# A transformer layer on one core: the first token block alone, from forgetting attention to its expert rows, under the other three; two dense expert blocks for three

## The chip, the cores and the metric

The kernel runs on one core of one Trainium2 chip. The metric is the device time in microseconds (us) of one execution. Before the change the median of three runs is 5321.05 us (5316.64 to 5322.71). The engines of a core are called as in its profile: PE (TensorE, matmuls; PEld is its weight load), DVE (VectorE), ACT (ScalarE), POOL (GpSimd) and SP (SyncE, which here only issues transfers).

## The reference

One layer over 512 tokens of 2048 features, in fp32, with a memory of 256 rows. Cut to what matters here:

```python
h = hybrid_mixer(x, w_in, ...)            # x @ w_in -> mLSTM (4 heads) and forgetting attention (16 heads of 128)
                                          # merged = sigmoid(g_ml) * (h @ w_br_ml) + sigmoid(g_fx) * (y @ w_br_fox)
                                          # return merged @ w_out
x = layer_norm(DN_ALPHA * x + h, ...)
h = memory_cross_attention(x, mem, w_q, w_kv, w_o)
x = layer_norm(DN_ALPHA * x + h, ...)
h = peer_ffn(x, w_pq, sub_keys, expert_u, expert_v)
x = layer_norm(DN_ALPHA * x + h, ...)

def peer_ffn(...):
    q = (x @ w_pq).reshape(B, S, PEER_HEADS, 2, PEER_DK // 2)       # 8 heads, two half keys
    sc = jnp.einsum('bshpd,hpnd->bshpn', q, sub_keys)               # 128 sub-keys each
    top_s, top_i = lax.top_k(sc, PEER_TOPK)                         # 16 + 16, then 16 of the 256 pairs
    ...
    def block(args):                                                # per block of 128 tokens
        a = jnp.einsum('tkd,td->tk', expert_u[it], xt)              # 8 * 16 = 128 experts a token
        hact = gelu(a) * gt
        return jnp.einsum('tk,tkd->td', hact, expert_v[it])
```

There are 128 x 128 = 16384 experts, each with one row of 2048 in `peer_u` and one in `peer_v` (128 MB a table). A token uses 128 of them. So a block of 128 tokens can be done in two ways: by gathering each token's own rows, or densely, with all 16384 experts and gates that are zero for those not chosen.

The forgetting attention is causal: the first 128 tokens need only the keys and values of the first 128. The mLSTM carries its state from the first token to the last.

## The kernel before

Tokens stand in four blocks of 128 (TB = 4). Weights come from memory in pieces of [128 x 1024] fp32, 512 KB, one `dma_start` on SP's queue each (`load_raw`, L116 to L119, tile `raw`, three buffers). Matmuls run in a rounded fp32 format; to keep precision, each weight piece is split in two (`split`, L110 to L114): ACT casts the high part (L111: `whi`, `vh`, `hph`), DVE subtracts it from the piece for the low part (L114: `wlo`, `vl`, `hpl`), or POOL does (L113), when the caller says so. `load_w` (L121) does load and split with two buffers each for `whi` and `wlo`. `mm3` (L128 to L131) multiplies with three matmuls: high by high (L129), and the two mixed products (L130, L131). Two functions use them for a group of 512 output features (eight pieces of weight): `group_ws` (L133) gives the features on the partitions and all tokens in the columns, 24 matmuls a piece; `group_as` (L147) gives a token block on the partitions and 512 features in the columns, 6 matmuls a piece and block.

The stages, in order: x and the gates; mLSTM (20 groups and its recurrence); forgetting attention (L354 on: 12 groups for queries, keys and values, `fox_head` at L358, four groups of gates, four of `w_br_fx`); `w_out` with norm 1 (L449 on), beside which the memory's keys and values are made (`w_xkv`, eight groups with 256 columns); the query groups and cross-attention; `w_xo` and norm 2; `peer_wq` with the selection (`top16` L619, `select` L628, `soften` L664).

Then the experts. Three token blocks (NDENSE = 384) are dense, the fourth is gathered.

- `stage_a(c)` (L785): gelu of `peer_u` by the dense tokens for first key c, 128 experts: two pieces `uT` of 512 KB and 48 matmuls of 384 columns. The first 52 run ahead (LOOK); most of the results wait in DRAM (`gad`).
- Beside these the gates are made as a dense array [second key, first key, token] (L705 to L745): in steps of four tokens, DVE compares the selected keys with a row of numbers (L724, L726, tiles of 128x512), POOL multiplies with the gate in two halves (L729), PE multiplies (L734), ACT and DVE copy and add the halves (L740, L741), and the result goes to DRAM (`gd`).
- `stage_h(c)` (L802): activation times gate (L813, tile `gb`), and its split (`hph`, `hpl`).
- `stage_o(c0, dh, fill)` (L842): J = 4 first keys at a time and one half of the 2048 output columns: four pieces of `peer_v` (tile `vh`, `vl`), 18 matmuls of 512 columns each into six PSUM banks, which DVE adds to the accumulators `acc` in SBUF (L879). Between these, `fill` starts the remaining `stage_a` and the gathers.
- The gathered block: each of 128 `gather_u` fetches with one indirect DMA on POOL's queue (L820) one row of `peer_u` for each of the block's 128 tokens, 1 MB, into `rows` (two buffers), and DVE multiplies and sums it with the token's features (L830); each `gather_v` does so with `peer_v` and adds the row times its factor to the accumulator (L839). u rows of one batch of eight and v rows of the batch before alternate. They are spread over the loop and tied to its pace by `pace` (L765).

The order of the instructions on each engine is chosen by the framework's scheduler, which simulates the program from the order in which it is written and the dependencies; there is no order written out by hand beside that and the `pace` ties. What a queue holds runs in its order: SP's queue carries the weight pieces, the gates and the output, POOL's carries its arithmetic and the gathers.

Of the kernel before, what the change touches and what calls it, by code (L numbers as in the profile page):

```python
# [21 lines left out]
P = 128  # L22
# [9 lines left out]
NDENSE = 384  # L32
# [4 lines left out]
# column groups of w_in, 512 columns each  # L37
# [6 lines left out]
def build(tc, I, out, dbg=None):  # L44
    nc = tc.nc
    dbg = dbg or {}
    with ExitStack() as ctx:
# [4 lines left out]
        apool = ctx.enter_context(tc.tile_pool(name="acts_a", bufs=1))  # L52
        phase_a = ctx.enter_context(ExitStack())
        bpool = phase_a.enter_context(tc.tile_pool(name="acts_b", bufs=1))
# [29 lines left out]
        # causal, transposed: [s, t] is one where t >= s  # L84
# [4 lines left out]
        # [q, k]: NEG where k > q  # L89
# [17 lines left out]
        lnbT = const_in("ln_bT", [P, 3, 16])  # L107

# [24 lines left out]
        def group_ws(src, X, n, evac, pool=False):  # L133
            """out^T of 512 features: evac(sub-block, bank [128 features, n tokens])."""
# [12 lines left out]
        def group_as(src, X, nt, evac):  # L147
            """512 features, tokens on partitions: evac(token block, bank [128 tokens, 512])."""
# [13 lines left out]
        def rstd(o, var, t):  # L162
            """o = (var + eps) ** -0.5, with one Newton step; t: two like columns of scratch."""
# [9 lines left out]
        # ================= x, gates =================  # L173
# [4 lines left out]
        with tc.tile_pool(name="gates", bufs=1, reuse_waits="tile") as gp:  # L178
# [21 lines left out]
            # log_sigmoid(z) = min(z, 0) - log1p(exp(-|z|))  # L200
# [4 lines left out]
            # log1p(e) = log(u) + (e - (u - 1)) / u  # L205
# [7 lines left out]
            # mLSTM: g = i - F, M = max(0, running max of g), m = F + M  # L213
# [15 lines left out]
        if "F" in dbg:  # L229
            nc.sync.dma_start(dbg["F"], sc_fx)  # L230
            nc.sync.dma_start(dbg["M"], sc_ml)

        wi = I["w_in"]

        # ================= mLSTM =================
        hT = []
        mg = dp.tile([16, P, S], F32, tag="mg", name="mg")
        with tc.tile_pool(name="ml", bufs=1, reuse_waits="tile") as mp:
            def mt(tag, bufs, shape=(P, 512)):
                return mp.tile(list(shape), F32, tag=tag, bufs=bufs, name=nm(tag))  # L240

            for h in range(ML_H):
# [59 lines left out]
                for tb in range(TB):  # L302
# [5 lines left out]
                    # r = 1 / max(|den|, exp(-m)); the head norm of num * r  # L308
# [23 lines left out]
            # sigmoid(g_ml) * (h @ w_branch_ml), transposed, to scratch  # L332
# [13 lines left out]
        if "mg" in dbg:  # L346
            nc.sync.dma_start(dbg["mg"], mg)
        if dbg.get("stop") == 1:
            return

        # ================= forgetting attention =================
        yT = []
        sgf = []
        with tc.tile_pool(name="fx", bufs=1, reuse_waits="tile") as fp:  # L354
            def ft(tag, bufs, shape=(P, 512)):
                return fp.tile(list(shape), F32, tag=tag, bufs=bufs, name=nm(tag))

            def fox_head(h, qT, kT, vts, off):  # L358
                nF = ft("nF", 2)
                nc.gpsimd.dma_start(nF, sc_fx[h].partition_broadcast(P))  # L360
                pr = []
                for qb in range(TB):
                    n = (qb + 1) * P
                    bank = sm_bank()
                    nc.tensor.matmul(bank[:, :n], qT[:, qb * P:n], kT[:, :n], start=True, stop=False)
                    nc.tensor.matmul(bank[:, qb * P:n], identb, maskb, start=False, stop=True)
                    p = fp.tile([P, n], F32, tag=f"p{qb}", bufs=1, name=nm("p"))
                    st = fp.tile([P, 4], F32, tag="st", bufs=8, name=nm("fst"))
                    nc.vector.tensor_tensor_reduce(out=p, in0=bank[:, :n], in1=nF[:, :n], scale=1.0, scalar=-3.0e38,
                                                   op0=ALU.add, op1=ALU.max, accum_out=st[:, 0:1])  # L370
                    nc.vector.tensor_scalar(st[:, 1:2], st[:, 0:1], -1.0, None, op0=ALU.mult)
                    nc.scalar.activation(p, p, AF.Exp, bias=st[:, 1:2], accum_out=st[:, 2:3])
                    nc.vector.reciprocal(st[:, 3:4], st[:, 2:3])
                    nc.vector.tensor_scalar(p, p, st[:, 3:4], None, op0=ALU.mult)
                    pr.append(p)
                pts = []
                for kb in range(TB):
                    bank = sm_bank()
                    for qb in range(kb, TB):
                        nc.tensor.transpose(bank[:, (qb - kb) * P:(qb - kb + 1) * P], pr[qb][:, kb * P:(kb + 1) * P],  # L380
                                            ident)
# [16 lines left out]
            for qd in range(4):  # L398
# [6 lines left out]
                def ev_k(s, b, ks=ks):  # L405
                    ks[s] = ft("c", 17)
                    nc.vector.tensor_copy(ks[s], b)
# [601 lines left out]
```

## Time and profile before

| | |
|---|---|
| median of three runs | 5321.05 us |
| the profiled execution's own span | 5323.6 us |
| PE busy | 5128.4 us, 24353 matmuls |
| DVE busy | 3192.8 us |
| ACT busy | 1594.5 us |
| POOL busy | 858.1 us |
| moved by DMA | 963.45 MB, 181 GB/s in the mean |

One execution on the chip was recorded. The page gives the busy time of each engine, slices of the span with the busy share in tenths, the DMA queues, the chain of work that ended last, and groups of instructions: line, engine, operation, tiles (written from read), shapes, their number, then busy time and the mean of one in ns, then the idle time of the engine just before them with what ended it. In a table of windows each row is a stretch of the span (from:to in us, length, then busy time and number of instructions for PE, PEld, DVE, ACT and POOL, the granted TensorE clock, the DMA share and GB/s). Ends of matmuls are modelled, and a matmul's mean includes what it overlaps with its neighbours, so its price is better read from a stretch in which PE never stops.

### The profile page before, as it was taken

The numbers are of one execution on the slowest core, as the hardware profiler recorded it, in microseconds if no ns is written. First come the engines' busy times: TensorE is split into PE (matmuls) and PEld (weight loads), VectorE is DVE, ScalarE is ACT, GpSimd is POOL, SyncE is SP. The second block draws the span as 40 slices with busy tenths as digits, with TensorE's granted clock in tenths as the row PEclk, the third lists the DMA queues.
The fourth block names the chain that finished last, engine by engine and source line by source line (L and its number), as shares of the span: only waits on it lengthen the run. The fifth ranks groups of instructions, "written<-read, shape, count | busy, mean of one in ns | idle before, by whom it ended". The sixth has DMA issues, their size and how long they took to land. (4 is left out here: it accounts for less than half of the span.)

```text
span 5323.6 us, 62349 instructions
## 1 busy us (share of the span) xinstructions
PE 5128.4 (96%) x24353; PEld 4366.2 (82%) x24353; DVE 3192.8 (60%) x4755; ACT 1594.5 (30%) x2260; POOL 858.1 (16%) x636
## 2 busy tenths in 40 slices
PE   9999999999999999999989978799999999999997
PEld 7777788877778888887878877788888888888886
DVE  4444322233332344632359999956888888888887
ACT  3322222222223222432232344333223332323232
POOL 0000000000000000500034544411122222222221
PEclk9999999999999999999999999999999999999998
DMA  3222233322222343632342344466888999999995
GB/s 132 86 89 84 87 111 107 108 87 91 90 89 89 113 135 127 207 126 75 100 141 84 118 138 143 157 226 233 323 326 330 341 325 337 331 333 334 336 342 207
DMA packets 295751, 963.45 MB, mean 181 GB/s; under 512 B 28604, under 2 KB 110076, under 8 KB 262304
## 3 DMA queue, kind: packets, MB, share of 16 engines
q1 hardware_dynamic: 178272, 597.37, 32.5%
q0 software_dynamic: 49552, 311.59, 15.9%
q10 hardware_dynamic: 67632, 50.50, 2.9%
q8 instruction: 191, 3.13, 0.2%
q14 instruction: 104, 0.85, 0.0%
HBM read 892.60 MB, written 66.76 MB: 180 GB/s over the span
## 5 line engine op out<-in xcount | busy, mean ns | idle before, releaser
L114 DVE TENSOR_TENSOR wlo<-raw,whi 128x1024 fp32r<-128x1024 f32 x748 | 978.4, 1308 | 1426.7 <-ACT whi L111 1399.7
L111 ACT CAST whi<-raw 128x1024 fp32r<-128x1024 f32 x768 | 809.9, 1055 | 2058.0 <-PE mm L130 868.4
L131 PE MATMUL pa<-Ah,wlo 128*128 128x384 f32 x2048 | 703.2, 343 | 80.0 <-DVE wlo L114 76.6
L129 PE MATMUL pa<-Ah,whi 128*128 128x384 f32 x2048 | 697.0, 340 | 19.4 <-ACT whi L111 16.9
L130 PE MATMUL mm<-Al,whi 128*128 128x512 f32 x1792 | 708.4, 395 | 3.6 <-DVE Al L114 3.6
L129 PE MATMUL mm<-Ah,whi 128*128 128x512 f32 x1792 | 707.7, 396 | 0.8 <-ACT whi L111 0.8
L130 PE MATMUL pa<-Al,whi 128*128 128x384 f32 x2048 | 695.5, 340 | 0.0
L131 PE MATMUL mm<-Ah,wlo 128*128 128x512 f32 x1792 | 677.6, 394 | 2.1 <-POOL wlo L113 1.6
L130 PE MATMUL po<-vl,hph 128*128 128x512 f32 x1536 | 602.2, 392 | 0.8 <-DVE vl L114 0.8
L131 PE MATMUL po<-vh,hpl 128*128 128x512 f32 x1536 | 600.7, 392 | 0.0
L129 PE MATMUL po<-vh,hph 128*128 128x512 f32 x1536 | 594.9, 391 | 4.3 <-ACT hph L111 2.7
L131 PEld LDWEIGHTS pa<-Ah,wlo 128*128 128x128 f32 x2048 | 391.5, 191 | 103.7 <-DVE wlo L114 97.1
L111 ACT CAST vh<-raw 128x1024 fp32r<-128x1024 f32 x256 | 269.4, 1053 | 631.4 <-DMA raw<-in_peer_v 444.3
L130 PE MATMUL mm<-wlo,Ah 128*128 128x512 f32 x1088 | 433.9, 399 | 0.3 <-DVE wlo L114 0.3
L131 PE MATMUL mm<-whi,Al 128*128 128x512 f32 x1088 | 424.0, 390 | 0.0
L129 PEld LDWEIGHTS pa<-Ah,whi 128*128 128x128 f32 x2048 | 391.8, 191 | 28.3 <-ACT whi L111 20.7
L130 PEld LDWEIGHTS mm<-Al,whi 128*128 128x128 f32 x1792 | 337.6, 188 | 81.1 <-issue 9.6
L131 PEld LDWEIGHTS mm<-Ah,wlo 128*128 128x128 f32 x1792 | 337.3, 188 | 75.1 <-POOL wlo L113 2.5
L129 PEld LDWEIGHTS mm<-Ah,whi 128*128 128x128 f32 x1792 | 337.9, 189 | 72.5 <-issue 1.7
L130 PEld LDWEIGHTS pa<-Al,whi 128*128 128x128 f32 x2048 | 391.3, 191 | 4.2
L129 PE MATMUL mm<-whi,Ah 128*128 128x512 f32 x1088 | 373.3, 391 | 0.7 <-ACT whi L111 0.7
L830 DVE SCALAR_TENSOR_TENSOR rows<-rows,x2l 128x2048 f32<-128x2048 f32 x128 | 292.9, 2289 | 130.9 <-DMA rows<-in_peer_u,ei 130.7
(297 smaller groups left out, 7477.9 us busy)
## 6 DMA issues: line engine op xcount, KB each, us to landing
raw<-in_w_in SPq DMA_DIRECT2D x256, 512.0 KB, 3.3
raw<-in_uT SPq DMA_DIRECT2D x256, 512.0 KB, 4.6
raw<-in_peer_v SPq DMA_DIRECT2D x256, 512.0 KB, 6.8
raw<-in_w_xkv SPq DMA_DIRECT2D x64, 512.0 KB, 3.3
gd<-stage ACTq DMA_DIRECT2D x12, 2048.0 KB, 13.4
G<-gd SPq DMA_DIRECT2D x64, 384.0 KB, 6.9
gad<-ga ACTq DMA_DIRECT2D x126, 192.0 KB, 4.8
gb<-gad SPq DMA_DIRECT2D x126, 192.0 KB, 6.2
```

What stands on the lines that cost most here:

```text
L111: nc.scalar.copy(hi, src)
L114: return nc.vector.tensor_sub(lo, src, hi.bitcast(F32))
L129: nc.tensor.matmul(o, wh, xh, start=first, stop=False)
L130: nc.tensor.matmul(o, wh, xl, start=False, stop=False)
L131: nc.tensor.matmul(o, wl, xh, start=False, stop=last)
L830: nc.vector.scalar_tensor_tensor(rows, rows, 1.0, x2l, op0=ALU.mult, op1=ALU.mult, accum_out=d[:, k % GB:k % GB + 1])
```

## The change

- The dense expert blocks are blocks 1 and 2 (`DENSE = (1, 2)`, NDENSE = 256). Blocks 0 and 3 are gathered.
- The memory's keys and values are made before the mLSTM and wait in DRAM.
- After the mLSTM, block 0 alone goes through forgetting attention, `w_br_fx`, `w_out`, norm 1, cross-attention, `w_xo`, norm 2, `peer_wq` and the selection. It loads the 36 groups of these stages (288 pieces) with `group_as` for one block, 6 matmuls of 512 columns a piece. Its keys and values of each head group wait in DRAM for the other blocks.
- Then the other three blocks go through the same 36 groups (384 columns in `group_ws`, three blocks in `group_as`), the pieces loaded a second time. With each of these pieces `load_w` issues 258/272 of a job of block 0's gathered expert part: one gather and its DVE product (all 128 of `peer_u`, then all 128 of `peer_v`, then the final norm). Each gather is tied to the split of the last piece. Every third split goes to POOL (`share=3`).
- The gates of the two dense blocks are built token by token: two DVE instructions on a [128 x 128] tile and one fp32 matmul a token, ACT copies the result; POOL has no part.
- `stage_a` runs with 256 columns; its first 20 first keys send their splits to POOL (before, the first four). In `stage_o` the two dense blocks take four banks, and the split of every third of four pieces goes to POOL. Block 3 is gathered in the loop with `rows` in three buffers, all u rows before the v rows, and starts after four first keys instead of eight.

The core of the diff (new or changed lines):

```diff
-NDENSE = 384
+DENSE = (1, 2)
+NDENSE = 128 * len(DENSE)
...
+        work = {"jobs": None, "rate": 0.0, "due": 0.0, "n": 0, "share": 0, "last": None}
...
-            split(hi, lo, raw, pool)
+            work["n"] += 1
+            if work["share"] and work["n"] % work["share"] == 0:
+                pool = True
+            work["last"] = split(hi, lo, raw, pool)
+            if work["jobs"] is not None:
+                work["due"] += work["rate"]
+                while work["due"] >= 1 and work["jobs"] is not None:
+                    work["due"] -= 1
+                    if next(work["jobs"], None) is None:
+                        work["jobs"] = None
             return hi, lo
...
+        def gather_rows(table, ei, k, last):
+            rows = gat.tile([P, D], F32, tag="rows", bufs=3, name=nm("rows"))
+            i = nc.gpsimd.indirect_dma_start(out=rows, out_offset=None, in_=I[table],
+                                             in_offset=bass.IndirectOffsetOnAxis(ap=ei[:, k:k + 1], axis=0))
+            after(i, last())
+            return rows
+
+        def gathered(t, xacc, ei, gg, last):
...
+            for k in range(P):
+                rows = gather_rows("peer_u", ei, k, last)
+                nc.vector.scalar_tensor_tensor(rows, rows, 1.0, xacc, op0=ALU.mult, op1=ALU.mult,
+                                               accum_out=dots[:, k:k + 1])
+                yield True
+            nc.scalar.mul(xacc, xacc, ALPHA)
+            nc.scalar.activation(dots, dots, AF.Gelu)
+            nc.vector.tensor_mul(dots, dots, gg)
+            for k in range(P):
+                rows = gather_rows("peer_v", ei, k, last)
+                nc.vector.scalar_tensor_tensor(xacc, rows, dots[:, k:k + 1], xacc, op0=ALU.mult, op1=ALU.add)
+                yield True
...
+            def proj(w, X, out, func=None, scale=1.0):
...
+                group_as(w, X, 1, ev)
+                return out
...
+            for qd in range(4):
+                tq = proj(wi[16 + 3 * qd], XA, big("tq"), scale=FX_D ** -0.5)
+                tk = proj(wi[17 + 3 * qd], XA, big("tk"))
+                vt = proj(wi[18 + 3 * qd], XA, big("vt"))
+                nc.gpsimd.dma_start(kvd[qd, 1], vt)
...
+        work.update(jobs=gathered(0, xacc0, ei0, gg0, lambda: work["last"]), rate=258 / 272, share=3)
...
+                group_ws(wi[16 + 3 * qd], XB, TR, ev_q)
+                group_ws(wi[17 + 3 * qd], XB, TR, ev_k)
+                group_as(wi[18 + 3 * qd], XB, 3, ev_v)
...
-                    nc.vector.tensor_tensor(o1, *i1, op=ALU.is_equal)
...
-                    nc.vector.tensor_tensor(e0, *i0, op=ALU.is_equal)
...
-                    nc.gpsimd.tensor_mul(o0, e0.unsqueeze(2).to_broadcast(f4),
-                                         gT[:, ta:ta + 4].bitcast(F32).unsqueeze(3).to_broadcast(f4))
...
+                    for u in range(4):
+                        c = slice(ta + u, ta + u + 1)
+                        o1 = gp.tile([P, P], F32, tag="o1", bufs=4, name=nm("o1"))
+                        nc.vector.tensor_scalar(o1, iota, selT["i1"][:, c], None, op0=ALU.is_equal)
+                        o0 = gp.tile([P, P], F32, tag="o0", bufs=4, name=nm("o0"))
+                        nc.vector.tensor_scalar(o0, iota, selT["i0"][:, c], selT["g"][:, c],
+                                                op0=ALU.is_equal, op1=ALU.mult)
+                        nc.tensor.matmul(bank[:, u * P:(u + 1) * P], o1, o0, start=True, stop=True)
...
-                uh, ul = load_w(I["uT"][c, kt], pool=c < 4)
+                uh, ul = load_w(I["uT"][c, kt], pool=c < 20)
...
-        LATE = 8          # first keys before the gathered block starts
+        LATE = 4
...
-                split(vh, vl, raw)
+                split(vh, vl, raw, pool=j == 2)
```

More of the change, by code (lines that the diff above doesn't have):

```diff
@@ new lines, in build, with fin_load, fin_stats @@
+        fst = {}
+        def fin_load(pool):
+            lw = []
+            for n in ("ln_w", "ln_b"):
+                t = pool.tile([P, D], F32, tag="rows", bufs=3, name=nm("lw"))
+                nc.gpsimd.dma_start(t, I[n][2].partition_broadcast(P))
+                lw.append(t)
+            return lw
+        def fin_stats(pool, t, acc, gs):
+            if t not in fst:
+                fst[t] = gat.tile([P, 32], F32, tag="fst", bufs=4, name=nm("fst"))
+            for g in gs:
+                nc.vector.bn_stats(fst[t][:, 6 * g:6 * g + 6], acc[:, g * 512:(g + 1) * 512])
@@ L694, in a_bank @@
+        work["share"] = 0
+        while work["jobs"] is not None:
+            if next(work["jobs"], None) is None:
+                work["jobs"] = None
         def a_bank():
@@ L727, in build @@
[L727 to L741 removed]
+                    bank = o_bank()
@@ L900, in fin @@
[L900 to L915 removed]
+                        fin(DENSE[t], acc[t], lwd)
```

841 lines of the change are left out of this document (457 added, 384 removed).

## The prediction

> **What bounds the kernel now.** I read the page first: its busy times and its slices.
>
> ```profile
> span 5323.6 us, 62349 instructions
> PE 5128.4 (96%) x24353; PEld 4366.2 (82%) x24353; DVE 3192.8 (60%) x4755; ACT 1594.5 (30%) x2260; POOL 858.1 (16%) x636
> DVE  4444322233332344632359999956888888888887
> GB/s 132 86 89 84 87 111 107 108 87 91 90 89 89 113 135 127 207 126 75 100 141 84 118 138 143 157 226 233 323 326 330 341 325 337 331 333 334 336 342 207
> ```
>
> PE is at 96%, but the slices show two halves: up to slice 20 DVE and the memory are mostly idle, in the last third both are near full. So I cut the span at the stage borders (the first weight cast of each stage) and asked for the windows: length, PE, PEld, DVE, ACT, POOL, granted clock, DMA share, GB/s.
>
> ```profile
> 0.00:945.00 945.00, 935.60 (x4097) 752.82 (x4098) 356.33 (x588) 259.04 (x306) 14.68 (x34) 1.00 0.29 99
> 945.00:1928.00 983.00, 983.00 (x4388) 792.37 (x4387) 346.05 (x609) 263.05 (x392) 18.30 (x34) 1.00 0.29 97
> 1928.00:2089.00 161.00, 160.05 (x706) 131.91 (x705) 60.80 (x69) 35.06 (x36) 8.60 (x16) 1.00 0.40 133
> 2089.00:2301.00 212.00, 201.16 (x1264) 181.57 (x1263) 128.52 (x132) 91.36 (x104) 74.66 (x60) 0.99 0.57 193
> 2301.00:2508.00 207.00, 207.00 (x886) 164.23 (x885) 61.31 (x86) 56.08 (x83) 0.00 (x0) 1.00 0.24 83
> 2508.00:2698.00 190.00, 190.00 (x830) 154.90 (x830) 62.52 (x76) 40.41 (x48) 6.46 (x12) 1.00 0.32 106
> 2698.00:2918.00 220.00, 202.22 (x935) 166.98 (x934) 180.89 (x607) 68.27 (x90) 105.11 (x80) 0.95 0.33 113
> 2918.00:3552.00 634.00, 534.76 (x2931) 500.46 (x2930) 563.32 (x1096) 249.25 (x561) 272.88 (x139) 0.97 0.46 151
> 3552.00:5293.00 1741.00, 1713.88 (x8328) 1520.63 (x8328) 1410.64 (x1458) 527.68 (x634) 347.17 (x259) 0.99 0.87 317
> 5293.00:5323.60 30.60, 0.76 (x4) 0.30 (x2) 22.46 (x43) 4.33 (x6) 10.24 (x3) 0.55 0.25 103
> ```
>
> They are mLSTM, forgetting attention, w_out, memory keys and values, query, w_xo, selection, look-ahead with gates, the expert loop, the tail. Up to 2918 PE bounds and DVE works a third of the time; the loop has PE, DVE and DMA at 98, 81 and 87%. Sums below stand against this span, 2.6 us (0.05%) above the median 5321.05.
>
> What a matmul costs is read where PE never stops, and with them the highest DMA rate and a stretch in which POOL works beside DVE:
>
> ```profile
> 1760.00:1920.00 160.00, 160.00 (x708) 132.53 (x707) 59.53 (x67) 37.94 (x44) 6.46 (x12) 1.00 0.37 116
> 2200.00:2222.00 22.00, 22.00 (x185) 22.00 (x185) 10.09 (x11) 8.38 (x8) 0.95 (x2) 1.00 0.73 255
> 3520.00:3555.00 35.00, 35.00 (x204) 35.00 (x203) 15.04 (x19) 11.44 (x16) 5.33 (x10) 1.00 1.01 369
> 2125.00:2215.00 90.00, 79.63 (x640) 77.64 (x639) 68.29 (x59) 40.08 (x50) 72.51 (x56) 0.98 0.64 216
> ```
>
> 512 columns: 160/708 = 0.226 us; 256: 22/185 = 0.119; 384: 35/204 = 0.172, while the memory gave 369 GB/s. Other prices are from the groups of instructions (mean ns of one behind the busy time), the DMA issues (us to landing last), and the loop's waits (us, times, longest):
>
> ```profile
> L111 ACT CAST whi<-raw 128x1024 fp32r<-128x1024 f32 x768 | 809.9, 1055 | 2058.0 <-PE mm L130 868.4 <-PE mm L131 627.1 <-DMA raw<-in_uT 244.0
> L114 DVE TENSOR_TENSOR vl<-raw,vh 128x1024 fp32r<-128x1024 f32 x256 | 311.2, 1219 | 39.3 <-ACT vh L111 33.1 <-PE pa L131 6.1
> L839 DVE SCALAR_TENSOR_TENSOR acc<-rows,dots,acc 128x2048 f32<-128x2048 f32 x128 | 300.6, 2348 | 89.4 <-DMA rows<-in_peer_v,ei 89.3
> L830 DVE SCALAR_TENSOR_TENSOR rows<-rows,x2l 128x2048 f32<-128x2048 f32 x128 | 292.9, 2289 | 130.9 <-DMA rows<-in_peer_u,ei 130.7
> L879 DVE TENSOR_TENSOR acc<-acc,po 128x512 f32<-128x512 f32 x372 | 238.6, 680 | 12.0 <-PE po L131 12.0
> L813 DVE TENSOR_TENSOR gb<-gb,G 128x384 f32<-128x384 f32 x126 | 69.0, 552 | 22.8 <-DMA gb<-gad 19.7 <-issue 2.4 <-DVE wlo L114 0.7
> L113 POOL TENSOR_TENSOR wlo<-raw,whi 128x1024 fp32r<-128x1024 f32 x20 | 47.9, 2393 | 29.4 <-ACT whi L111 29.3
> L374 DVE TENSOR_SCALAR p<-p,fst 128x128 f32<-128x128 f32 x16 | 4.6, 287 | 0.6
> ```
> ```profile
> raw<-in_w_in SPq DMA_DIRECT2D x256, 512.0 KB, 3.3
> raw<-in_peer_v SPq DMA_DIRECT2D x256, 512.0 KB, 6.8
> rows<-in_peer_u,ei POOLq DMA_INDIRECT x128, 8.8
> ```
> ```profile
> POOL rows L820 <- DVE rows L830: 618.5, 115, 9.6
> ACT vh L111 <- DMA raw<-in_peer_v: 444.3, 141, 8.2
> ```
>
> **The change, part by part.**
>
> *Memory keys and values first.* The 64 loads leave the norm beside which they ran: 384 matmuls with 512 columns and 768 with 256 are 384×0.226 + 768×0.119 = 178 us; with 12 us for the spill and the border (my choice; 0 to 30), behind 945: **1135**.
>
> *Block 0 alone.* 36 groups, 288 loads, six matmuls each: 288×6×0.226 = 391 us of PE. It is no longer PE that bounds: a buffer of the load ring (three) is taken for a landing, a cast and a subtraction, (3.3 + 1.06 + 1.22)/3 = 1.86 us a load, 536 us as the low end; the high end is the memory stage's pace, 178/64 = 2.8 us, 806. Waits for the two whi and wlo buffers lie between; I take 2.2 us, nearer the ring, 634, and 26 for two norms and a selection that nothing covers: **660**.
>
> *The other three blocks, gathers beside them.* The stages from 945 to 2918 less the memory's 212 last 1761 us, of which 36×192×0.226 = 1562 are weight matmuls and 199 the rest. Now 24 groups run at 384 columns (24×192×0.172 = 793), twelve with three blocks (12×144×0.226 = 391), three quarters of the rest (149), and norm 1 without cover (212 − 178 = 34): PE 1367. DVE: 256 row products at 2.32 are 594, 191 of the 288 subtractions at 1.22 are 233 (97 go to POOL), the rest is three quarters of 375 (711.6 in these five windows, less 276 subtractions), of 50 for norm 1 and of 64 for selection work of the next window: 367. Sum 1194. POOL has 97×2.39 = 232 and 80 of norms and selection: 310 us.
>
> What POOL's work costs DVE is the open price. The stretch from 2125 in detail, and the look-ahead's subtractions:
>
> ```profile
> L114 DVE TENSOR_TENSOR wlo<-raw,whi 128x1024 fp32r<-128x1024 f32 x25 | 39.9, 1603 | 20.7 <-ACT whi L111 20.7
> L114 DVE TENSOR_TENSOR Al<-pT,Ah 128x512 fp32r<-128x512 f32 x16 | 21.3, 1361 | 0.0
> L114 DVE TENSOR_TENSOR wlo<-raw,whi 128x1024 fp32r<-128x1024 f32 x95 | 168.2, 1772 | 32.2 <-ACT whi L111 31.9
> ```
>
> There 25 subtractions grew from 1.22 to 1.60 and 16 of 512 columns from 0.68 (the nearest row, L879) to 1.36: 20.5 us lost beside 72.5 of POOL, 0.28 per POOL us. The other end is 1.0, POOL and DVE taking turns; I take 0.6, between them, because POOL's and DVE's long instructions here both read two tiles of SBUF: 186. A gather's product waited 220/256 = 0.86 us for its rows in the loop, with two buffers; with three I take half, 110. So DVE has 1194 + 186 + 110 = 1490, above PE's 1367; I take **1500**. The weights (151 MB), gathers (270) and the rest (36) need 457 MB, 1240 us at 369 GB/s, 1442 at the loop's 317: not the bound unless slower. Ends: 1367 (nothing lost, PE) and 1724 (price 1.0, whole waits). Each POOL split stands behind the gathers issued before it, and those behind a product that frees a row buffer: load ring, then PE, wait for that. The ring pays this from its slack of 1500/288 = 5.2 us a load against 4.24 in the loop (12.7 us round a buffer, landings at 6.8); without it a late split is a late load. Block 0's two output stores stand on SP's queue among the last loads, some us each.
>
> *Look-ahead and gates.* 2496 matmuls of 256 columns, 297 us. The multiply on POOL and the wide comparisons go; 512 comparisons of 128x128 at 0.287 are 147, 64 subtractions at 1.22 to 1.77 with the spilled selection 161: DVE 308. The 256 matmuls per token are fp32 of 128 columns, as these were:
>
> ```profile
> L685 PE MATMUL sm<-keysT,qT 128*128 128x128 f32 x128 | 16.2, 275 | 0.2 <-ACT sc L688 0.2
> L365 PE MATMUL sm<-c,c 128*128 128x512 f32 x32 | 16.5, 598 | 0.0
> ```
>
> At most 0.275 each, 70 us; by the columns alone (598 − 275 over 384 columns, times 128) 0.108, 28 us. So PE has 325 to 367, about the same as DVE's 308 at the present share of the busier engine (563/634 = 0.89), 346. I take **360**; range 325 to 450, the upper end with 40 POOL splits (96 us) turned into DVE time in full.
>
> *The loop.* DVE's 1410.6 and 220 of waits; less 124 accumulator additions ×0.68 (84, five more elsewhere: 79), a quarter of twice L813's 69 us (34: the gate multiply and the subtraction of the same shape go from 384 columns to 256, and short instructions fall less than in proportion: 0.287 at 128 columns in L374) and 64 splits (78) that go to POOL as 153 us ×0.6 = 92; waits halved: 1421. At the present fullness of PE, 1714/1741, less a margin, 0.94: 1512. DMA: 317×1741 = 552 MB less 20 of spills and gates, 532: 1442 us at 369, 1565 at 340. PE falls to 3072×0.226 + 3648×0.119 = 1128, so it no longer covers late landings: I take the DMA's **1565**, range 1450 to 1741. Block 3's product order changes too, all rows of the first table before those of the second; the traffic is the same, so I cost it at nothing; if one table's rows land later, the waits that I halved come back, 110 us.
>
> *Tail*: **31**, the last norm unchanged.
>
> Sum: 1135 + 660 + 1500 + 360 + 1565 + 31 = 5251, **5250**: before the experts +377 (3295 against 2918), look-ahead −274, loop −176.
>
> **Rivals.**
>
> *Nothing waits (chance 0.23).* Block 0 at 2.0 us (600), the second pass at 1420 near PE, look-ahead 335, loop 1500: 5021. For it: DVE's waits came with two buffers. Against: it needs every stage at its bound.
>
> *Slower: POOL's work takes DVE's time in full (0.22).* The place is the second pass and the loop, 463 us of POOL splits and the like. At price 1.0 instead of 0.6 the second pass takes 124 more, the loop 61/0.94 = 65: 5440. Each tenth is 47 us; it decides at 0.75. For it: the look-ahead's subtractions stood at 1.77 instead of 1.22; against: 0.28 in the other stretch. The Trainium skill ("SBUF — State Buffer", section "Who interferes with whom") says that a VectorE instruction with two SBUF inputs contends with a GpSimd one that reads SBUF and that the shared port is an exclusive lock, the loser blocked fully. By that rule the price is 1.0 and the time this rival's; the trace agrees as to the contention (1603 and 1772 ns), not with its full size.
>
> *The loop does not shrink (0.10).* The ring and the gather stream paced it, not PE: its casts waited 444 us for landings. Then 1741, sum 5427; equal to before at 1638. Against: a third fewer matmuls and adds, 64 fewer DVE splits, and 20 MB less.
>
> That the change does what it says is no rival: the built program has the block-0 products between the second pass's loads.
>
> **How the numbers follow.** Forecast 0.45 (5150 to 5310, the bounds of look-ahead and loop), then 0.23, 0.22, 0.10. The range 5030 to 5480 leaves out half of the deep case and the far end of the slower ones. A measurement tells 0.2%, 11 us. Faster: 0.23 and most of the forecast, 0.40 = 0.63; same 0.05; slower 0.32.
>
> The Trainium skill ("HBM Reference", "Specifications (TRN2)") puts a core streaming alone at about 425 GB/s; the row's best is 369. By it the loop's DMA needs 1252 and DVE's 1512 bounds: 5198, inside the forecast.
>
> **What would show it.** Right: block 0's loads about 2.2 us apart with PE 60% busy; the second pass at DVE over 90% with PE over 85%; its subtractions at 1.5 us or more; the loop with DMA near 1.0 and PE near 70%. Wrong: subtractions at 1.22 beside busy POOL (price near 0) or casts waiting on POOL splits, which in turn wait on gathers; PE idle in the second pass for landings above 8.8 us; a loop whose casts wait as long as before; a look-ahead in which PE never stops while DVE does; a block 0 above 2.8 us a load.

## The result, and the profile after

The changed kernel takes 5595.73 us (median, 5586.16 to 5600.56) against 5320.87: a ratio of 1.0509, interval 1.0493 to 1.0525. It is 5.1% slower where 1.3% faster was forecast, and lies outside the range. From the page of the changed kernel:

```profile
span 5597.3 us, 64707 instructions
PE 4813.2 (86%) x24366; PEld 4068.8 (73%) x24366; DVE 3771.2 (67%) x5101; ACT 1851.8 (33%) x2426; POOL 1604.0 (29%) x1108
GB/s 207 171 88 87 85 85 104 113 194 239 239 225 213 232 345 333 328 307 322 346 235 292 323 241 144 150 187 248 317 322 324 323 322 320 303 338 325 307 314 251
```

PE has 315 us less to do than before, and the end still comes 274 us later: no engine is near full over the span any more. The stages, cut as in the prediction (up to the end of mLSTM, block 0 alone, the other three blocks, look-ahead with gates, expert loop, tail; columns as before):

```profile
0.00:1156.00 1156.00, 1132.00 (x5312) 932.13 (x5313) 447.14 (x671) 337.98 (x396) 23.52 (x51) 0.99 0.36 117
1156.00:1886.00 730.00, 552.91 (x2081) 372.39 (x2079) 448.74 (x632) 361.79 (x434) 71.01 (x93) 0.94 0.73 227
1886.00:3448.00 1562.00, 1405.22 (x7196) 1264.72 (x7195) 1220.14 (x1561) 472.43 (x673) 840.40 (x572) 0.96 0.81 296
3448.00:3903.00 455.00, 395.75 (x3029) 382.00 (x3028) 329.61 (x966) 176.40 (x305) 126.86 (x68) 0.94 0.57 185
3903.00:5571.00 1668.00, 1321.52 (x6731) 1113.03 (x6730) 1308.66 (x1242) 498.02 (x615) 536.58 (x324) 0.89 0.85 317
5571.00:5597.30 26.30, 5.83 (x26) 4.50 (x24) 16.87 (x31) 5.22 (x6) 5.60 (x2) 0.68 0.20 80
```

| stage | before | forecast | after | after less forecast |
|---|---|---|---|---|
| to the end of mLSTM, with memory | 945 (without) | 1135 | 1156 | +21 |
| block 0 alone | | 660 | 730 | +70 |
| the other blocks (before: all blocks, 945 to 2918) | 1973 | 1500 | 1562 | +62 |
| look-ahead and gates | 634 | 360 | 455 | +95 |
| expert loop | 1741 | 1565 | 1668 | +103 |
| tail | 31 | 31 | 26 | −5 |
| sum | 5324 | 5251 | 5597 | +346 |

Up to the experts the kernel pays 530 us more than before (3448 against 2918); the look-ahead gives 179 back, the loop 73, the tail 4. Two readings matter. The loop moves 317 GB/s, exactly as before, though PE has a fifth fewer matmuls there (6731 records against 8328) and DVE 100 us less. And in block 0's stage nothing is full: PE 76%, DVE 61%, DMA 73%. In both, the three raw buffers are the suspect. The loop's landings, from the DMA issues of that stretch (the last column is the median us from issue to landing),

```profile
raw<-in_peer_v SPq DMA_DIRECT2D x254, 512.0 KB, 6.7
raw<-in_uT SPq DMA_DIRECT2D x152, 512.0 KB, 6.1
```

make 406 loads in 1668 us, 4.11 us each, so 12.3 us round one of three buffers; before it was 12.8. The loop's waits (us, times, longest) show both ends of such a round. The casts wait for pieces to land, 645 us in all (687 before), while SP's queue holds the next piece back until a subtraction has read the old one and its buffer is free:

```profile
ACT vh L116 <- DMA raw<-in_peer_v: 381.2, 175, 9.0
ACT whi L116 <- DMA raw<-in_uT: 263.3, 105, 9.5
```
```profile
SPq L123 <- DVE vl L119: 341.8, 142, 9.1
SPq L123 <- DVE wlo L119: 295.6, 114, 10.5
SPq L123 <- POOL vl L118: 196.9, 50, 9.2
```

### The profile page after: what moved, and what is told of

Read it like the earlier page. It is cut to its first block, busy times and chain, and to the rows that moved or that the text cites. A ratio compares the mean times of both kernels' runs of the same rounds, so it can differ in the third digit from the quotient of the medians.

```text
span 5597.3 us, 64707 instructions
## 1 busy us (share of the span) xinstructions
PE 4813.2 (86%) x24366; PEld 4068.8 (73%) x24366; DVE 3771.2 (67%) x5101; ACT 1851.8 (33%) x2426; POOL 1604.0 (29%) x1108
## 5 line engine op out<-in xcount | busy, mean ns | idle before, releaser
L579 DVE SCALAR_TENSOR_TENSOR xacc<-rows,dots,xacc 128x2048 f32<-128x2048 f32 x256 | 650.6, 2541 | 145.9 <-DMA rows<-in_peer_v,ei 144.2
L147 PE MATMUL pa<-Ch,wlo 128*128 128x256 f32 x2048 | 622.8, 304 | 141.8 <-DVE wlo L119 128.1
L571 DVE SCALAR_TENSOR_TENSOR rows<-rows,xacc 128x2048 f32<-128x2048 f32 x256 | 630.1, 2467 | 123.7 <-DMA rows<-in_peer_u,ei 123.4
L145 PE MATMUL pa<-Ch,whi 128*128 128x256 f32 x2048 | 613.9, 300 | 37.4 <-ACT whi L116 31.9
L146 PE MATMUL pa<-Cl,whi 128*128 128x256 f32 x2048 | 609.8, 298 | 0.0
L145 PE MATMUL mm<-Ah,whi 128*128 128x384 f32 (+1 forms) x1536 | 552.8, 360 | 3.2 <-DVE t L825 3.2
L146 PE MATMUL mm<-Al,whi 128*128 128x384 f32 (+1 forms) x1536 | 550.3, 358 | 0.0
L147 PEld LDWEIGHTS pa<-Ch,wlo 128*128 128x128 f32 x2048 | 419.7, 205 | 160.2 <-DVE wlo L119 141.8
L147 PE MATMUL mm<-Ah,wlo 128*128 128x384 f32 (+1 forms) x1536 | 497.5, 360 | 22.2 <-DVE wlo L119 16.1
L145 PEld LDWEIGHTS pa<-Ch,whi 128*128 128x128 f32 x2048 | 419.5, 205 | 49.2 <-ACT whi L116 38.5
```

The lines of the kernel that those rows point to most:

```text
L145: nc.tensor.matmul(o, wh, xh, start=first, stop=False)
L146: nc.tensor.matmul(o, wh, xl, start=False, stop=False)
L147: nc.tensor.matmul(o, wl, xh, start=False, stop=last)
L571: nc.vector.scalar_tensor_tensor(rows, rows, 1.0, xacc, op0=ALU.mult, op1=ALU.mult, accum_out=dots[:, k:k + 1])
L579: nc.vector.scalar_tensor_tensor(xacc, rows, dots[:, k:k + 1], xacc, op0=ALU.mult, op1=ALU.add)
```

## The experiments

My theory after this reading: the ring of three raw buffers (each is taken for a landing, a cast and a subtraction, with waits between, before it can take the next piece) paces block 0's stage and the expert loop; the second pass and the look-ahead are held by PE and by what GpSimd's splits do. The rivals: the memory gives no more than 317 GB/s beside gathers; VectorE is full; the row buffers of the gathers pace the loop.

A kernel's ratio is to the kernel before on the same chip; its stages are read from its own profile, where the border between look-ahead and loop is the first cast of a `peer_v` piece. It moves when loads run further ahead (the look-ahead takes 377 us instead of 455 in some runs below, with more of `stage_a` left to the loop), so for the loop the time from the look-ahead's start to the end counts, 2149 us in the changed kernel. In runs that change nothing behind that point it is 2136 to 2161.

### More raw buffers from the look-ahead on

```diff
+        more = {"pool": None, "bufs": 0, "n": 0}
...
-            raw = wp.tile([P, 1024], F32, tag="raw", bufs=3, name=nm("raw"))
+            more["n"] += 1
+            if more["n"] % (3 + more["bufs"]) < more["bufs"]:
+                raw = more["pool"].tile([P, 1024], F32, tag="rawx", bufs=more["bufs"], name=nm("raw"))
+            else:
+                raw = wp.tile([P, 1024], F32, tag="raw", bufs=3, name=nm("raw"))
...
         acc = [mn.tile([P, D], F32, tag=f"acc{t}", name=f"acc{t}") for t in range(NT)]
+        more.update(pool=mn, bufs=4)
```

> The ring of raw weight pieces has seven buffers in the expert loop instead of three; nothing else changes. Theory (the ring of three, a landing of 6.9 us and a split, paces the loop at 4.1 us a load): the loop's 1672 us fall to 1400 to 1550, where VectorE's 1310 us and its waits end it, the whole to about 5350 to 5450; landings stay under 8 us. Rival (the memory gives no more than the 316 GB/s seen there): the loop stays within 40 us of 1672, and the landings of a piece double to 12 us or more.

5505.7 us, ratio 1.0342 (1.0320 to 1.0363): the whole misses the theory's 5350 to 5450. The loop's weights ended after 1268 us instead of 1668, at 358 GB/s, so memory was not at its limit at 317. But the look-ahead grew from 455 to 533 us, and the last product of gathered rows ended 228 us after the last cast of a weight. So the pace of the gathered rows stood behind the ring, and the look-ahead's weights had a new wait: SP's queue stood 195 us for the stores of the gates (`gd<-stage`) there.

### The ring in the loop alone, the row buffers alone, both

The same helper, set at the loop's start:

```diff
+        more.update(pool=mn, bufs=4)
+        rn.update(bufs=1)
         for c0 in range(0, NC_, J):
```

where `rn` does for the gathered `rows` what `more` does for `raw` (four buffers instead of three). Both lines:

> Of all changes only the loop's: seven raw buffers and four row buffers, used from the loop's start on, so that the look-ahead keeps its three. Theory (the look-ahead's 80 us more with seven buffers were its weights waiting for memory that the gates build still held): look-ahead 455 as before, loop 1370 to 1450, the whole 5300 to 5380. Rival (the time only moves between the two stages): their sum stays at the 2065 that seven buffers from the look-ahead on gave, the whole at 5500.

5345.74 us, ratio 1.0032 (1.0016 to 1.0047). From the look-ahead's start to the end it takes 1904 us instead of 2149: 245 us of the loss, with nothing else changed. In its loop the casts wait 33 us for landings instead of 645:

```profile
ACT whi L116 <- DMA raw<-in_uT: 23.1, 8, 6.5
ACT vh L116 <- DMA raw<-in_peer_v: 9.5, 5, 3.3
```

Only the row buffer (`bufs=0` in the first line):

> The loop with four buffers of gathered rows and the three raw buffers of the changed kernel. If the ring of raw pieces paces the loop: it stays within 25 us of 1672. If the row buffers do (GpSimd's gathers waited 510 us for products to free one): it falls to 1500 or less.

5623.37 us, ratio 1.0580 (1.0558 to 1.0601): nothing gained. Only the raw buffers (without the second line):

> The loop with seven raw buffers, used from its start on, and three row buffers. If the ring alone paces the loop: loop and tail fall from 1690 to about the 1522 that both gave. If both pace it in turn: the weights run ahead and the gathered rows end 100 to 250 us after them, loop and tail 1580 to 1640.

5424.27 us, ratio 1.0206 (1.0184 to 1.0228): loop and tail take 1598 us instead of 1694. The windows, of the row buffer alone first (the loop), then of the raw buffers alone (loop, and the gathers after it), then of both:

```profile
3899.00:5593.00 1694.00, 1330.43 (x6733) 1116.25 (x6732) 1306.17 (x1242) 497.65 (x615) 520.79 (x324) 0.89 0.82 312
```
```profile
3808.00:5154.00 1346.00, 1251.93 (x7306) 1085.29 (x7305) 1165.06 (x1190) 512.38 (x651) 429.25 (x259) 0.99 0.94 351
5154.00:5406.00 252.00, 6.53 (x28) 4.75 (x26) 189.38 (x121) 6.56 (x8) 103.25 (x74) 0.53 0.82 305
```
```profile
3818.00:5284.00 1466.00, 1297.41 (x7306) 1118.24 (x7305) 1301.26 (x1251) 513.59 (x651) 607.22 (x320) 0.95 0.95 365
```

So the ring paces the loop, and the row buffers pace it as soon as the ring doesn't: a row buffer more is worth nothing with three raw buffers, and some 75 us with seven (1980 against 1904 us from the look-ahead's start). With both, DMA is busy 95% at 365 GB/s: only there the memory comes near to being the bound, which my forecast took it for from the outset.

### The loop without block 3's rows

```diff
+SKIP = (3,)
...
-            for k in range(P):
+            n_rows = P if t not in SKIP else 0
+            if n_rows == 0:
+                nc.vector.memset(dots, 0.0)
+            for k in range(n_rows):
                 rows = gather_rows("peer_u", ei, k, last)
...
-            for k in range(P):
+            for k in range(n_rows):
                 rows = gather_rows("peer_v", ei, k, last)
```

This kernel leaves block 3's expert part out of the output.

> The changed kernel with block 3's 256 gathers and products left out (its expert part is missing from the output). Theory (the ring of three paces the loop, through landings that the gathers lengthen to 6.9 us and a split that waits 2 us behind their products): a landing falls to 4 to 5 us, the wait to under 1, a load from 4.1 to 2.8 us, the loop to 1130 to 1250. If the ring with its GpSimd splits paced it by itself: above 1400.

5135.02 us, ratio 0.9641 (0.9618 to 0.9664). Window of the loop, and landings in it:

```profile
3892.00:5106.00 1214.00, 1161.33 (x6724) 1021.96 (x6723) 697.48 (x844) 482.90 (x609) 153.45 (x64) 0.99 0.66 211
```
```profile
raw<-in_peer_v SPq DMA_DIRECT2D x254, 512.0 KB, 4.6
raw<-in_uT SPq DMA_DIRECT2D x152, 512.0 KB, 4.2
```

Landings fall by 2 us, a load from 4.11 to 2.99 us, and PE becomes the bound at 96%. So 256 gathers and their products cost the loop 454 us. They do it through the landings of the weights and, as far as the waits show, through the low parts that come later: TensorE waits 260 us for these in the changed kernel's loop and 20 here.

### GpSimd's splits: second pass, loop, look-ahead

```diff
-        work.update(jobs=gathered(0, xacc0, ei0, gg0, lambda: work["last"]), rate=258 / 272, share=3)
+        work.update(jobs=gathered(0, xacc0, ei0, gg0, lambda: work["last"]), rate=258 / 272, share=0)
```

> No split of the second pass goes to GpSimd (share 0). My forecast's theory (VectorE bounds this pass, GpSimd's work costs it 0.6 us per us): VectorE takes 96 subtractions of 1.22 more, 117 us, and loses 139 us less to the port: the pass, 1561 us, moves by less than 30. Rival (the pass is bound by TensorE, and late GpSimd splits behind the gathers stop it): TensorE's waits for the low parts fall by 40 us or more and the pass comes to 1480 to 1520. Second rival (VectorE is needed for the products and gets too full): the pass grows to 1600 or more.

5507.28 us, ratio 1.0333 (1.0310 to 1.0356): the pass takes 1480 us instead of 1562, as the first rival said; VectorE's theory falls. Its window, then VectorE's groups in that pass, without the GpSimd splits and as changed:

```profile
1892.00:3372.00 1480.00, 1382.70 (x7197) 1255.02 (x7196) 1224.26 (x1613) 478.01 (x677) 555.62 (x473) 0.97 0.84 312
```
```profile
L119 DVE TENSOR_TENSOR wlo<-raw,whi 128x1024 fp32r<-128x1024 f32 x288 | 367.2, 1276 | 94.4 <-ACT whi L116 89.2 <-PE mm L147 2.8 <-ACT fpt L442 1.6
L579 DVE SCALAR_TENSOR_TENSOR xacc<-rows,dots,xacc 128x2048 f32<-128x2048 f32 x128 | 306.4, 2394 | 53.8 <-DMA rows<-in_peer_v,ei 53.4
L571 DVE SCALAR_TENSOR_TENSOR rows<-rows,xacc 128x2048 f32<-128x2048 f32 x128 | 292.4, 2286 | 43.2 <-DMA rows<-in_peer_u,ei 43.0
```
```profile
L579 DVE SCALAR_TENSOR_TENSOR xacc<-rows,dots,xacc 128x2048 f32<-128x2048 f32 x128 | 335.7, 2622 | 102.7 <-DMA rows<-in_peer_v,ei 101.8
L571 DVE SCALAR_TENSOR_TENSOR rows<-rows,xacc 128x2048 f32<-128x2048 f32 x128 | 327.1, 2558 | 97.4 <-DMA rows<-in_peer_u,ei 97.3
L119 DVE TENSOR_TENSOR wlo<-raw,whi 128x1024 fp32r<-128x1024 f32 x193 | 251.9, 1305 | 70.6 <-ACT whi L116 70.5
```

VectorE makes 95 subtractions more (115 us) and is busy 4 us longer. So GpSimd's splits, 285 us of its time (840 against 556), had relieved VectorE of next to nothing: its products had grown from 2286 and 2394 ns to 2558 and 2622, 64 of the 111 us, and the rest lies in its other work. The splits stand on one queue with the gathers and took 2821 ns each:

```profile
L118 POOL TENSOR_TENSOR wlo<-raw,whi 128x1024 fp32r<-128x1024 f32 x96 | 270.8, 2821 | 161.5 <-ACT whi L116 149.8 <-issue 5.7 <-PE mm L146 5.2
L561 POOL DMA_INDIRECT rows<-in_peer_u,ei x128 | 197.9, 1546 | 240.1 <-DVE wlo L119 84.2 <-DVE rows L571 72.9 <-issue 36.2
```

TensorE's waits in the pass say how most of the 82 us divide. As changed, it waits 39 us for low parts from GpSimd and 54 for those from VectorE, the longest single waits at GpSimd's:

```profile
PE mm L147 <- DVE wlo L119: 34.5, 24, 4.3
PE mm L147 <- POOL wlo L118: 32.0, 9, 12.9
```

Without the splits these are none and 35, so 58 us less, and TensorE is busy 22 us less for the same matmuls, at a granted clock of 0.97 instead of 0.96. VectorE's waits for rows halve too, from 199 to 96 us.

In the loop:

```diff
-                split(vh, vl, raw, pool=j == 2)
+                split(vh, vl, raw, pool=False)
```

> No split of the expert loop goes to GpSimd; nothing else changes. If the load ring paces the loop, a GpSimd split (2.64 us, and its wait behind the gathers) in every fourth expert-value piece costs the ring more than a VectorE split: the loop falls by 20 to 60 us from 1672. If VectorE bounds it, 64 subtractions of 1.25 come on top: 80 us more. If the memory bounds it: within 20 us.

5549.26 us, ratio 1.0432 (1.0396 to 1.0467); loop and tail fall by 32 us, within what the ring theory gave. In the look-ahead:

```diff
-                uh, ul = load_w(I["uT"][c, kt], pool=c < 20)
+                uh, ul = load_w(I["uT"][c, kt], pool=c < 4)
```

> The changed kernel, of the look-ahead's splits only those of four first keys on GpSimd instead of twenty. If these splits are the cause of the look-ahead's 95 us over the forecast: look-ahead and loop together fall by 40 to 70 us, as they did by 61 with the deeper buffers. If that gain needed the deeper buffers, because the ring paces the loop here: 20 to 35, from the look-ahead alone.

5564.86 us, ratio 1.0464 (1.0446 to 1.0481): the look-ahead falls by 19 us, the loop not at all. VectorE's groups there, as changed and without these splits:

```profile
L977 DVE TENSOR_SCALAR o<-iota,i0T,gT 128x128 f32<-128x128 f32 x256 | 111.6, 437 | 0.0
L975 DVE TENSOR_SCALAR o<-iota,i1T 128x128 f32<-128x128 f32 x256 | 79.1, 310 | 15.5 <-PE po L979 14.8
```
```profile
L119 DVE TENSOR_TENSOR wlo<-raw,whi 128x1024 fp32r<-128x1024 f32 x96 | 120.8, 1260 | 83.7 <-ACT whi L116 83.7
L977 DVE TENSOR_SCALAR o<-iota,i0T,gT 128x128 f32<-128x128 f32 x256 | 86.9, 341 | 0.0
L975 DVE TENSOR_SCALAR o<-iota,i1T 128x128 f32<-128x128 f32 x256 | 71.5, 281 | 10.4 <-PE po L979 10.0
```

Again VectorE has 32 subtractions more (42 us) and is not busier (329.6 and 325.8 us).

### The second pass without block 0's rows

The same edit for block 0 (`SKIP = (0,)`), whose expert part is then missing from the output:

> Block 0's 256 gathers and their products are left out of the second pass (its expert part is missing from the output); the splits still go to GpSimd every third time. If TensorE bounds that pass and the gathers only disturb it: 1561 falls to 1390 to 1470, TensorE's 1367 and the norms. If VectorE's products were the bound: VectorE falls by 660 us and the pass all the way to TensorE's 1370 or less. If the GpSimd splits cost without gathers ahead of them as well: it stays above 1500.

5466.46 us, ratio 1.0276 (1.0253 to 1.0300): the pass takes 1414 us, PE 97% busy:

```profile
1894.00:3308.00 1414.00, 1368.64 (x7196) 1252.95 (x7195) 602.25 (x1230) 469.80 (x668) 404.37 (x317) 0.98 0.40 135
```

The 256 gathers and products cost it 148 us there, against 454 in the loop.

### The gates' fp32 matmuls

```diff
-                        nc.tensor.matmul(bank[:, u * P:(u + 1) * P], o1, o0, start=True, stop=True)
-                    bv = bank.rearrange("p (t c) -> p c t", t=4)
+                        if u == 0:
+                            nc.tensor.matmul(bank[:, :P], o1, o0, start=True, stop=True)
+                    bv = bank[:, :P].unsqueeze(2).to_broadcast([P, P, 4])
```

One matmul in four is left, and its result stands for the other three tokens, whose gates are wrong.

> Of the fp32 matmuls that build the gates one in four is left, its result copied four times (the gates of three tokens in four are wrong); the comparisons on VectorE stay. If these matmuls stand in TensorE's way in the look-ahead (455 us, 100 us in their records): it falls by 60 to 80 us. If VectorE's comparisons (191 us) or the chain through ACT's copies sets it: less than 20.

5575.05 us, ratio 1.0480 (1.0447 to 1.0514): the look-ahead takes 449 us instead of 455, while TensorE is busy 36 us less. These matmuls, 100 us of records in the changed kernel's look-ahead (two records each), are not what holds it:

```profile
L979 PE MATMUL po<-o,o 128*128 128x128 f32 x512 | 100.4, 287 | 6.3 <-DVE o L977 5.6
```

### Block 0 alone with more buffers

Three raw buffers more in this stage, given up again before the selection:

```diff
+            rx = ExitStack()
+            more.update(pool=rx.enter_context(tc.tile_pool(name="rx", bufs=1, reuse_waits="tile")), bufs=3)
...
+            more.update(pool=None, bufs=0)
+            rx.close()
             with tc.tile_pool(name="topa", bufs=1, reuse_waits="tile") as tp:
```

> The ring of raw pieces has six buffers instead of three while block 0 goes alone up to its selection; nothing else changes. Theory (that stage is paced by the ring at 7.6 us round a buffer): its 730 us fall to 560 to 640, where the two whi and wlo buffers and TensorE's six matmuls end it, the whole to about 5430 to 5510. Rival (the chain cast, subtraction, matmuls over two buffers paces it already): the stage stays within 20 us of 730 and the pieces wait, landed, for their cast.

5490.86 us, ratio 1.0317 (1.0292 to 1.0343). The stage falls from 730 to 640 us, the upper end of what the ring theory gave. The casts' waits for landings fall from 188 to 11 us, and their waits for matmuls, which still read the `whi` buffers, grow from 100 to 211: the next ring, of two buffers, takes over:

```profile
1154.00:1794.00 640.00, 520.02 (x2078) 361.24 (x2077) 442.48 (x631) 360.32 (x434) 70.54 (x92) 0.97 0.78 259
```

### Together

Block 0's raw buffers, no GpSimd splits in the second pass and the loop, and deeper buffers in the loop, allotted from the look-ahead on:

> Together: six raw buffers while block 0 goes alone, no GpSimd splits in the second pass and in the loop, and in the loop seven raw buffers and four buffers of gathered rows instead of three. If the single gains add up (about 90, 105, 85 and 45): 5595 less 325, some 5270, faster than the kernel before by 1%. If the gathered rows set the end of the loop once the weights run ahead (the stream ended 260 us before the end with seven buffers): the loop gains nothing beyond the 90, and the sum is 5310 to 5340.

5241.63 us, ratio 0.9859 (0.9839 to 0.9880): 354 us less than the changed kernel, a little more than the 330 of the four single edits (without the row buffer), and 1.4% faster than the kernel before. With five raw and five row buffers:

> As the one with seven raw and four row buffers, but five raw and five row buffers in the loop. If the gathered rows set the loop's end there, one row buffer more moves the end forward by 40 us or more against it; if the weight ring does, two raw buffers fewer cost 20 us or more.

5367.34 us, ratio 1.0089 (1.0071 to 1.0108): the loop needs the raw buffers. The look-ahead had grown to 540 and 551 us in these two. With the deeper buffers used from the loop's start on:

> As the one with everything together (seven raw and four row buffers), but these used from the loop's start on only. Theory: look-ahead 455 instead of 540, loop as there (1365), the whole 5140 to 5190. Rival (moved only): within 25 us of 5242.

5181.65 us, ratio 0.9732 (0.9710 to 0.9753): the look-ahead's wait was real time, not a moved border. From the look-ahead's start to the end this takes 1904 us, as with the deeper buffers alone, so leaving out GpSimd's splits in the loop added nothing there. And with only the splits of four first keys on GpSimd in the look-ahead:

> As the last, and of the look-ahead's splits only those of the first four first keys go to GpSimd, not twenty. If GpSimd's splits slow VectorE's comparisons there by the shared port (437 and 310 ns instead of 287): about 40 us of VectorE's come back and 39 go there again for the 32 splits, so within 15 us. If late GpSimd splits hold TensorE (30 us of its waits): 20 to 40 us faster. If VectorE, over 90% busy in the first 150 us, sets the look-ahead: 30 to 50 us slower.

5116.93 us, ratio 0.9605 (0.9585 to 0.9625): **4% faster than the kernel before**, the fastest version. The gain of 65 us is above what was expected and above what the same edit brought the changed kernel (1.0509 to 1.0464, some 25 us). Why the loop moves 384 GB/s here and 370 without this edit stays open. Its stages, as in the table above, without the tail of 52 us:

```profile
0.00:1155.00 1155.00, 1131.62 (x5313) 931.92 (x5314) 447.15 (x671) 337.77 (x397) 23.50 (x51) 0.99 0.36 117
1155.00:1796.00 641.00, 520.07 (x2077) 361.55 (x2077) 442.31 (x631) 360.02 (x434) 70.73 (x92) 0.97 0.79 259
1796.00:3276.00 1480.00, 1384.68 (x7196) 1255.58 (x7195) 1220.56 (x1613) 478.30 (x676) 555.76 (x474) 0.97 0.84 312
3276.00:3690.00 414.00, 368.14 (x2916) 357.49 (x2915) 325.46 (x1027) 170.05 (x294) 54.26 (x31) 0.96 0.58 184
3690.00:5066.00 1376.00, 1227.22 (x6846) 1053.75 (x6845) 1276.60 (x1299) 491.73 (x621) 447.86 (x260) 0.97 0.99 384
```

Last, block 0's stage with four raw and three `whi` and `wlo` buffers instead of six and two:

> Everything together as before (deeper buffers in the loop, no GpSimd splits but the first four first keys), and in block 0's stage four raw and three whi and wlo buffers instead of six and two. If the two buffers of cast, subtraction and matmuls hold what the ring left (2.14 us a load): the stage falls to 560 to 600, where VectorE's subtraction and TensorE's 1.36 us end it. If the ring still does: four raw buffers are too few and the stage grows from 640 to 680 or more.

5142.20 us, ratio 0.9665 (0.9648 to 0.9683). The stage takes 638 us, as with six raw buffers: neither branch of the expectation. The waits show the two rings trading places: the casts wait 64 us for matmuls and 153 for landings, where it was 211 and 11 with six raw and two `whi` buffers. Whether both rings opened together would bring the stage below 2.2 us a load, no run shows.

## Why the prediction was wrong

- *The step that failed most is the loop's pace* (1565, measured 1668; 103 of the 346 us over the forecast). "PE falls … so it no longer covers late landings: I take the DMA's **1565**" took the memory as the loop's next bound, at 340 GB/s. Three raw buffers give 317, before and after. The 12.7 us round a buffer, which the prediction spent only as slack of the second pass, prove nothing by themselves: they are three times the loop's time per load. The sign was in the waits: before the change the casts already waited 687 us for landings (444 of them shown with the prediction), and a loop that waits so shrinks only as its landings and waits do. The prediction's own sign of being wrong, "a loop whose casts wait as long as before", came, with 645. The rival "the loop does not shrink" was right in its mechanism and got 0.10; its 1741 was measured as 1668, with a round shorter by half a us. Its "a third fewer matmuls and adds" holds for `stage_o` alone; all matmuls of the loop are a fifth fewer. That the ring is the cause is shown: four raw buffers more brought 169 us (2149 to 1980), with the row buffer 245; the row buffer alone none.
- *Block 0 alone* (660, measured 730): the mechanism was right, the ring, and the term that was too small is the landing: 3.3 us, read in stages that moved 97 to 99 GB/s. When the loads come one after another at 227 GB/s, they land as in these rows of that stretch:

```profile
raw<-in_w_in SPq DMA_DIRECT2D x127, 512.0 KB, 4.4
raw<-in_w_xo SPq DMA_DIRECT2D x32, 512.0 KB, 4.3
```

  The casts there come 2.36 us apart in the median, not 2.2, and seven pauses of more than 5 us make 64 us together, where 26 were added for norms and selection. Six buffers bring 640, near the forecast of 660 by another kernel than the one forecast.
- *The other blocks* (1500, measured 1562): the sum came near for a wrong reason. VectorE was to be full with 1490 us; it was busy 1220 and waited 199 for rows. Its subtractions took 1305 ns, not the 1.5 us or more that was to show it. TensorE was the nearest bound, busy 1405 us, 1367 forecast and 1369 measured without gathers. GpSimd's price on VectorE was 0.39 a GpSimd us, not 0.6: the 285 us of splits took back 111 of the 115 us that they saved. They cost the pass 82 us on another path, TensorE's waits for low parts (58) and 22 us more of its busy time, at a lower clock. The slower rival had the place but not the mechanism. The Trainium skill ("SBUF — State Buffer", section "Who interferes with whom") calls the port an exclusive lock, the loser blocked for the whole instruction. The trace agrees with the contention, not with a full us of loss per us: the splits are GpSimd's time with two reads, and VectorE lost 0.39 of it.
- *Look-ahead* (360, measured 455): the comparisons, taken at 287 ns, cost 437 and 310 beside GpSimd and 341 and 281 without most of it: 44 us too little with, 12 without. The forecast left TensorE, with 325 to 367 us of work, next to no wait, while VectorE's 308 was divided by 0.89; TensorE was busy 396 and idle 59. GpSimd's splits account for 19 us of the stage; the matmuls, taken as 28 to 70, showed 100 in their records, and three quarters of them hold only 6 us. The raw ring does not pace this stage, since the casts wait 6 us for landings in it. What the rest of the 95 is, no run told apart.
- *Memory first* (1135, measured 1156): the 64 loads themselves took 178 us as forecast (first to last cast: 37 to 216 us in the trace); the rest is the border and the start, 21 us more than my 12.
- *Right*: PE's fall in the second pass, the gathers mostly hidden there (148 us for 256), the tail.

The forecast was that resources bound each stage. In the changed kernel none of them does in block 0's stage, the look-ahead and the loop. With deeper buffers and most of GpSimd's splits left out, DMA is busy 99% in the loop of the fastest version, and the time comes 2.5% below the forecast; that is another kernel, and does not confirm the forecast.

## What to carry to other kernels

Before a stage is costed by its engines and bytes, work out its ring: buffers over (landing + cast + subtraction + waits) gives the loads that can pass at all, and casts that wait for landings show that it is the pace. Such a stage gains little from what is taken off the engines: it shrinks only as its landings and waits do. Landings must be taken at the rate that the changed stage will have. Work that is handed to an idle engine is not relief if it slows the one relieved and comes late from a queue of transfers that wait. And where a change thins an engine's work, give the buffers that pace the stream more room; here the deeper buffers and the return of most splits to VectorE together turned 5% slower into 4% faster.

## What the runs showed of the hardware that was not expected

In the loop the granted clock fell with PE's idle time: 0.89 at 79% busy, 0.99 with seven raw buffers at 93%. The busy share alone doesn't set it, since block 0's stage had 0.94 at 76%. The loop's matmuls took longer at the lower clock: 1322 us of PE for 6731 matmuls against 1252 for 7306. The Trainium skill ("TensorE: Matmul & The Clock Gate", Part 1: The HAM clock gate) says that throttled is the default state and that activity releases it; the traces agree as to the direction, 0.53 in the 252 us in which only gathers are left.
